# Moving the adds of the SwiGLU weight-block sums from VectorE to GpSimd in a hybrid conv/RWKV-7 trunk

## The chip, the cores and the metric

One core of a Trainium2 chip. The metric is the device time of one launch in microseconds, as the median of three runs. The kernel computes in 32-bit floats; large products run on TensorE as three passes over operands that are split in a high and a low part.

## The reference, cut to what matters

One layer (DEPTH = 1) over 2048 prompt tokens and 64 decode tokens. The part that the change touches belongs to the feed-forward network at the end:

```python
proj = jnp.einsum('btd,dc->btc', h, p["w_in"])            # input projection, 42 blocks of 128 columns
...
x = x + _rms_norm(m, p["norm_mix_post"])
h = _rms_norm(x, p["norm_ffn_pre"])
up = jnp.einsum('btd,df->btf', h, p["w_ffn_up"])
f = jnp.einsum('btf,fd->btd', jax.nn.silu(up[..., :D_FF]) * up[..., D_FF:], p["w_ffn_down"])
x = x + _rms_norm(f, p["norm_ffn_post"])
```

Between the projection and the feed-forward network stand a short gated convolution, an RWKV-7 recurrence over chunks of 64 tokens, and the merge of the two branches.

## The kernel before, in words

The kernel has two phases. Phase A (`phase_a`) makes the input projection and, woven into it, the RWKV-7 scan. The projection goes through the tokens in slices of 264 columns, two at a time; every weight block of `w_in` (128 x 1024 floats, 512 KB) is loaded by SP into `w_raw` (two buffers), cast by ACT into `w_hi` (L149) and reduced by DVE to `w_lo` (L150), and then used for 48 matrix products (8 row blocks, 3 passes, two token slices). What comes out of PSUM is worked on by ACT, DVE and POOL: in `rwkv_unit` POOL copies one column of history into the row tile `pr` (L303) and the last column back (L305), and DVE mixes each token with its predecessor (L307). The scan's three streams (`scan_prep`, `scan_solve`, `scan_chain`) use small DVE instructions (L759 and L761 solve triangular systems, L703, L704 and L715 make their inputs), 64-wide matrix products (`pu`, `pa`, `gy`, `tr`) and two POOL instructions for each group (L861, L862). Phase B merges the branches and runs the SwiGLU network.

The feed-forward products use a scheme with seven block products in the place of eight. Some of these need sums and differences of weight blocks. `weight_sums` makes them during phase A: for each of 34 jobs (22 of `w_up`, 12 of `w_down`) SP loads four blocks into the four buffers `sw` (L602), four adds in place make the four sums (L605), and SP stores them to the DRAM scratch `us_s` or `ds_s` (L609), from where phase B reads them. 88 of the 136 blocks belong to `w_up`; 120 adds have 512 columns, 16 have 384. The job's steps are called from `projections` through `sum_step`, from the 24th call on at every second call.

Nothing in the text fixes the final order: the framework's scheduler sets the rows of each engine from the written order, the buffers and its own estimates; on the chip each engine then works through its rows in that order, waiting on semaphores. SP's rows carry nearly all loads and stores of phase A, the weight blocks (L148), the loads and stores of the sums (L602, L609), the scratch stores (L380) and the scan's loads (L650) among them. A row that waits holds up all behind it on its engine.

Of the kernel before, what the change touches and what calls it, by code (L numbers as in the profile page):

```python
# [13 lines left out]
ALU = mybir.AluOpType  # L14
# [71 lines left out]
class Trunk:  # L86
# [500 lines left out]
    def weight_sums(self):  # L587

        nc = self.nc
        up, wd = self.i["w_up"], self.i["w_down"]  # L590
        jobs = [(lambda i, j, f=f: up[NF * i + f, :, HK * j:HK * j + HK, :], lambda s, f=f: self.us_s[s, f]) for f in range(NF)]
        for u in range(4):
            for k0, kn in KCHUNKS:
                jobs.append((lambda i, j, u=u, k0=k0, kn=kn: wd[2 * u + i, :, FH * j + k0:FH * j + k0 + kn, :],
                             lambda s, u=u, k0=k0, kn=kn: self.ds_s[s, u, :, k0 * P:(k0 + kn) * P]))
        for src, dst in jobs:
            w = {}
            for i in range(2):
                for j in range(2):
                    x = src(i, j)  # L600
                    w[i, j] = self.pa.tile([P, HK, P], F32, name="sw", bufs=4)[:, :x.shape[1]]
                    nc.sync.dma_start(out=w[i, j], in_=x)  # L602
            yield
            for n, (x, y) in enumerate((((1, 1), (1, 0)), ((1, 0), (0, 0)), ((0, 0), (1, 1)), ((0, 1), (0, 0)))):
                nc.vector.tensor_tensor(out=w[x], in0=w[x], in1=w[y], op=ALU.add)  # L605
                if n % 2:
                    yield
            for k, sm in (((1, 1), S_1), ((1, 0), S_3), ((0, 0), S_2), ((0, 1), S_4)):
                nc.sync.dma_start(out=dst(sm), in_=w[k].rearrange("p k c -> p (k c)"))  # L609
            yield  # L610
# [854 lines left out]
```

## Time and profile before

| | us |
|---|---|
| median of 3 runs (lowest to highest) | 3318.92 (3309.05 to 3333.54) |
| the profiled execution, its own time | 3331.18 |
| span of the profiled execution | 3329.4 |
| busy in the span: PE, DVE, ACT, POOL | 3145.9, 2497.7, 1663.1, 463.7 |
| mean granted TensorE clock | 0.974 of 2.4 GHz |

Times within the execution are microseconds from the start of the span. Phase A's projection and scan reach to about 1480 us; the sums lie between 26 and 1176 us. Busy times are unions; "idle before" and "waited for" name what ended a wait. The chain is the sequence of work and waits that ended last, followed back in time. The profiled execution lies 12 us above the median of the runs, so differences are worked out against 3331.18 and then put on 3318.92.

### The profile page before, as it was taken

How to read it: one execution, taken by the hardware profiler on the slowest of the kernel's cores; microseconds unless marked ns; L12 is line 12 of the kernel's file. 1: busy time of each engine (PE TensorE's matmuls, PEld its weight loads, DVE VectorE, ACT ScalarE, POOL GpSimd, SP SyncE). 2: the span in 40 equal slices, each digit the busy share in tenths (PEclk: the TensorE clock that was granted, in tenths of full speed). 3: DMA queues.
4: the chain of work that ended last, by engine and by line, in shares of the span. 5: the costliest groups of instructions: out<-in, count | busy, mean ns of one | idle time of the engine just before them, and what ended most of it. 6: DMA issues, size and time to landing. Idle time of an engine off the chain costs nothing.

```text
span 3329.4 us, 64336 instructions
## 1 busy us (share of the span) xinstructions
PE 3145.9 (94%) x23060; PEld 3061.0 (92%) x23060; DVE 2497.7 (75%) x5325; ACT 1663.1 (50%) x3246; POOL 463.7 (14%) x885
## 2 busy tenths in 40 slices
PE   5899998999989999998998999999999999999996
PEld 5889998988988899998998999999999999999996
DVE  6776887888778876745486788886878887877766
ACT  6534664565476445443434355346544456444453
POOL 2310022032013100000010011210012200111100
PEclk9999999999999999999999999999999999999998
DMA  7787677766675655547475467778767777766674
GB/s 259 239 247 228 203 245 235 246 195 210 175 237 164 205 147 172 157 141 228 126 229 162 137 218 235 259 224 269 231 220 239 248 246 240 234 191 192 194 233 147
DMA packets 534833, 699.52 MB, mean 210 GB/s; under 512 B 112672, under 2 KB 368224, under 8 KB 534512
## 3 DMA queue, kind: packets, MB, share of 16 engines
q1 hardware_dynamic: 478880, 597.27, 59.1%
q0 software_dynamic: 24000, 67.61, 5.4%
q10 hardware_dynamic: 31632, 30.53, 2.7%
q8 instruction: 181, 2.97, 0.4%
q14 instruction: 140, 1.15, 0.1%
HBM read 522.10 MB, written 173.12 MB: 209 GB/s over the span
## 4 chain that ended last, share of the span: by engine, by line
issue 42%; PE 35%; DMA 8%; DVE 7%; POOL 5%; ACT 2%; SPq 0%; POOLq 0%; ACTq 0%; DVEq 0%
PE mm L136 28%; PE pu L136 4%; POOL tp_s L1214 3%; PE gy L136 2%; DMA w_raw<-in_w_in 1%; DVE w_lo L150 1%; PE tr L140 1%; DMA x<-in_x 1%; POOL x_s L1085 1%; DMA lo_s<-ks 1%; POOL out_y L1085 1%; DVE sw L605 1%; PE pa L136 1%; DVE ti L761 1%; DMA ka<-lo_s 1%
## 5 line engine op out<-in xcount | busy, mean ns | idle before, releaser
L136 PE MATMUL mm<-h_hi,w_hi 128*128 128x264 f32 (+1 forms) x5112 | 1594.9, 312 | 53.5 <-DVE f L1233 22.7
L136 PE MATMUL mm<-h_lo,w_hi 128*128 128x264 f32 (+1 forms) x5112 | 1567.2, 307 | 4.3 <-DVE h_lo L217 3.6
L136 PE MATMUL mm<-h_hi,w_lo 128*128 128x264 f32 (+1 forms) x5112 | 1563.5, 306 | 7.0 <-DVE w_lo L150 7.0
L136 PEld LDWEIGHTS mm<-h_hi,w_hi 128*128 128x128 f32 x5112 | 978.9, 192 | 80.9 <-DVE f L1233 26.8
L136 PEld LDWEIGHTS mm<-h_lo,w_hi 128*128 128x128 f32 x5112 | 981.3, 192 | 9.4 <-DVE h_lo L217 4.7
L136 PEld LDWEIGHTS mm<-h_hi,w_lo 128*128 128x128 f32 x5112 | 980.7, 192 | 8.8 <-DVE w_lo L150 7.8
L188 ACT CAST w_hi<-w_raw 128x512 fp32r<-128x512 f32 (+1 forms) x810 | 485.7, 608 | 587.9 <-PE mm L136 435.1
L189 DVE TENSOR_TENSOR w_lo<-w_raw,w_hi 128x512 fp32r<-128x512 f32 (+1 forms) x810 | 540.6, 674 | 145.8 <-ACT w_hi L188 140.4
L136 PE MATMUL mm<-t_hi,w_hi 128*128 128x352 f32 x1116 | 361.1, 324 | 0.6 <-ACT o L1058 0.6
L136 PE MATMUL mm<-t_hi,w_lo 128*128 128x352 f32 x1116 | 358.3, 321 | 0.0
L136 PE MATMUL mm<-t_lo,w_hi 128*128 128x352 f32 x1116 | 358.2, 321 | 0.0
L150 DVE TENSOR_TENSOR w_lo<-w_raw,w_hi 128x1024 fp32r<-128x1024 f32 x168 | 208.3, 1240 | 96.6 <-ACT w_hi L149 94.6
L149 ACT CAST w_hi<-w_raw 128x1024 fp32r<-128x1024 f32 x168 | 175.8, 1047 | 157.5 <-PE mm L136 126.5
L136 PEld LDWEIGHTS mm<-t_hi,w_hi 128*128 128x128 f32 x1116 | 209.4, 188 | 1.3 <-ACT o L1058 0.8
L136 PEld LDWEIGHTS mm<-t_lo,w_hi 128*128 128x128 f32 x1116 | 209.9, 188 | 0.3
L136 PEld LDWEIGHTS mm<-t_hi,w_lo 128*128 128x128 f32 x1116 | 209.4, 188 | 0.0
L1214 POOL DMA_DIRECT2D tp_s<-f x231 | 124.9, 541 | 574.4 <-DVE f L1233 327.9
L189 DVE TENSOR_TENSOR t_lo<-d,t_hi 128x352 fp32r<-128x352 f32 x198 | 97.6, 521 | 85.7 <-ACT t_hi L188 85.1
L188 ACT CAST t_hi<-d 128x352 fp32r<-128x352 f32 x198 | 90.9, 485 | 110.5 <-DMA d<-tp_s 103.8
L1233 DVE TENSOR_TENSOR f<-mm,f 128x352 f32<-128x352 f32 x198 | 103.1, 521 | 47.7 <-PE mm L136 47.4
L759 DVE TENSOR_TENSOR tm<-al,ti 128x60 f32<-128x60 f32 (+27 forms) x527 | 118.7, 225 | 17.1 <-DMA ti<-in_eye 5.1
L761 DVE TENSOR_TENSOR ti<-ti,tm 128x60 f32<-128x60 f32 (+27 forms) x527 | 123.7, 235 | 9.8
(198 smaller groups left out, 3747.3 us busy)
## 6 DMA issues: line engine op xcount, KB each, us to landing
w_raw<-in_w_in SPq DMA_DIRECT2D x168, 512.0 KB, 4.3
w_raw<-us_s SPq DMA_DIRECT2D x264, 256.0 KB, 3.1
w_raw<-in_w_up SPq DMA_DIRECT2D x198, 256.0 KB, 3.4
tp_s<-f POOLq DMA_DIRECT2D x231, 176.0 KB, 3.6
d<-tp_s SPq DMA_DIRECT2D x105, 352.0 KB, 4.0
w_raw<-ds_s SPq DMA_DIRECT2D x96, 256.0 KB, 3.7
sw<-in_w_up SPq DMA_DIRECT2D x88, 256.0 KB, 4.4
us_s<-sw SPq DMA_DIRECT2D x88, 256.0 KB, 3.7
```

The source lines that it names most:

```text
L136: self.nc.tensor.matmul(out, lhsT, rhs, **kw)
L140: self.nc.tensor.transpose(out, in_, ident)
L149: nc.scalar.copy(out=hi[:, :kt], in_=raw[:, :kt])
L150: nc.vector.tensor_tensor(out=lo[:, :kt], in0=raw[:, :kt], in1=hi[:, :kt].bitcast(F32), op=ALU.subtract)
L188: nc.scalar.copy(out=hi, in_=x)
L189: (eng or nc.vector).tensor_tensor(out=lo, in0=x, in1=hi.bitcast(F32), op=ALU.subtract)
L605: nc.vector.tensor_tensor(out=w[x], in0=w[x], in1=w[y], op=ALU.add)
L759: nc.vector.tensor_tensor(out=tv, in0=al[0:np_, u, u + 1:32].unsqueeze(1).broadcast_to([np_, k, m]), in1=ti[0:np_, 0:k, u:u + 1].broadcast ...
L761: nc.vector.tensor_tensor(out=tu, in0=tu, in1=tv, op=ALU.add)
L1085: (nc.sync if tail else nc.gpsimd).dma_start(out=dst[d, :, t0:t0 + n], in_=x)
L1214: nc.gpsimd.dma_start(out=self.tp_s[TP[op], i], in_=x)
L1233: nc.vector.tensor_tensor(out=out, in0=x, in1=y, op=op)
```

## The change

The adds of L605 are issued on POOL (GpSimd) and no longer on DVE (VectorE):

```diff
             for n, (x, y) in enumerate((((1, 1), (1, 0)), ((1, 0), (0, 0)), ((0, 0), (1, 1)), ((0, 1), (0, 0)))):
-                nc.vector.tensor_tensor(out=w[x], in0=w[x], in1=w[y], op=ALU.add)
+                nc.gpsimd.tensor_tensor(out=w[x], in0=w[x], in1=w[y], op=ALU.add)
                 if n % 2:
                     yield
```

The scheduler answers with another order on every engine. On POOL, at the start of phase A (`acc` and `hf` belong to the norm of the second token slice, `pr` is the row tile, `sw` the sums):

```order
 L184 TENSOR_TENSOR acc<-acc,psv 128x264 x7
+L605 TENSOR_TENSOR sw<-sw 128x512 x4
 L215 TENSOR_TENSOR hf<-kbk,rs 128x264 x2
...
-L215 TENSOR_TENSOR hf<-al,rs 128x264 x3
...
+L215 TENSOR_TENSOR hf<-al,rs 128x264 x2
+L605 TENSOR_TENSOR sw<-sw 128x512
+L215 TENSOR_TENSOR hf<-al,rs 128x264
+L605 TENSOR_TENSOR sw<-sw 128x512 x3
+L305 COPY pr_hist<-pr 128x1
```

The first four adds now stand between the sums of squares and the scaling of the second slice, and the next four ahead of the first copies of history.

On SP, at the same place, before:

```order
L194 DMA x<-in_x 128x2x264 x3
L609 DMA us_s<-sw 128x512
L148 DMA w_raw<-in_w_in 128x1024 x2
L609 DMA us_s<-sw 128x512 x3
L602 DMA sw<-in_w_up 128x512 x4
L296 DMA ka<-lo_s 128x264
```

and on SP after the change:

```order
L194 DMA x<-in_x 128x2x264 x3
L609 DMA us_s<-sw 128x512 x4
L602 DMA sw<-in_w_up 128x512 x2
L148 DMA w_raw<-in_w_in 128x1024 x2
L602 DMA sw<-in_w_up 128x512 x2
L609 DMA us_s<-sw 128x512 x4
```

The pair of weight loads that stood behind one store of a sum stands behind four stores and two of the next loads.

On POOL in the later part of the first passes (`cc` is the decay that the state update reads, `tinv` the inverse of the solve), before:

```order
L772 MEMSET tinv 32x16x32
L724 COPY cc<-ep 128x4 x2
L665 MEMSET ep 128x8
L861 TENSOR_TENSOR ysq<-ysq,bv 128x512
L862 TENSOR_TENSOR ysq<-ysq,g 128x512
```

and after the change:

```order
L772 MEMSET tinv 32x16x32
L861 TENSOR_TENSOR ysq<-ysq,bv 128x512
L862 TENSOR_TENSOR ysq<-ysq,g 128x512
L605 TENSOR_TENSOR sw<-sw 128x512 x12
L724 COPY cc<-ep 128x4
L605 TENSOR_TENSOR sw<-sw 128x512 x2
L724 COPY cc<-ep 128x4
```

Here the adds of three jobs stand in one run ahead of a copy that the state update waits for. Over the whole program all 136 adds stand on POOL, in 49 rows, 15 of them runs of four; of the 168 loads of `w_in` blocks, 101 stand ahead of the last store of a sum on SP, where 132 did.

## Rows read from the trace of the kernel before

**Rows 1.** Busy time by stretch: us, PE, PEld, DVE, ACT, POOL (instructions), clock, DMA, GB/s.
```profile
0.00:166.00 166.00, 123.80 (x877) 117.15 (x878) 117.41 (x193) 101.31 (x209) 51.31 (x95) 0.95 0.77 249
166.00:500.00 334.00, 317.53 (x2840) 304.01 (x2839) 249.66 (x607) 173.87 (x320) 44.05 (x89) 0.97 0.75 231
500.00:832.00 332.00, 309.79 (x2701) 295.12 (x2699) 281.94 (x688) 188.05 (x375) 79.20 (x146) 0.95 0.73 221
832.00:1210.00 378.00, 356.11 (x3222) 337.20 (x3221) 292.85 (x783) 204.36 (x409) 71.09 (x161) 0.95 0.64 192
1210.00:1480.00 270.00, 268.82 (x2473) 257.12 (x2472) 182.42 (x470) 141.12 (x247) 15.01 (x20) 1.00 0.52 154
```

**Rows 2.** What PE waited for from 45 to 1210 us: total, times, longest.
```profile
PE tr L140 <- DMA v<-v_s: 14.5, 3, 8.1
PE pu L136 <- DVE aa L715: 13.1, 16, 2.3
PE pa L136 <- DVE v L704: 11.0, 7, 2.4
PE mm L136 <- DVE w_lo L150: 7.0, 4, 3.8
```

**Rows 3.** Line 605: durations in ns (min/median/max), and DVE's idle time ahead of it.
```profile
L605 DVE TENSOR_TENSOR sw<-sw x136: 543/684/1791, 25.9 to 1175.7; 128x512 f32<-128x512 f32 x120, 128x384 f32<-128x384 f32 x16
...
  DMA sw<-in_w_up: 11.0, 5
...
  DMA sw<-in_w_down: 2.5, 1
```

**Rows 4.** The chain that ended last, from 0 to 1210 us, shares by line.
```profile
by line: PE mm L136 41.1%; PE pu L136 8.4%; issue 5.8%; PE gy L136 3.1%; DMA w_raw<-in_w_in 2.4%; DVE w_lo L150 2.2%; PE tr L140 1.9%; DMA lo_s<-ks 1.8%; DMA x<-in_x 1.8%; DVE sw L605 1.7%; DVE ti L761 1.6%; DMA ka<-lo_s 1.6%; DMA us_s<-sw 
```

**Rows 5.** POOL's instruction groups over the span: busy us, mean ns, idle before.
```profile
L861 POOL TENSOR_TENSOR ysq<-ysq,bv 128x512 f32<-128x512 f32 (+1 forms) x17 | 24.1, 1415 | 189.7 <-ACT ysq L860 115.9 <-PE mm L136 62.3 <-DVE sw L605 11.4
L862 POOL TENSOR_TENSOR ysq<-ysq,g 128x512 f32<-128x512 f32 (+1 forms) x17 | 23.8, 1402 | 1.3
```

**Rows 6.** Timeline from 363.5 us: start, us, engine, line, operation.
```profile
363.76 0.19 DVE L761 TENSOR_TENSOR ti<-ti,tm 128x28 f32<-128x28 f32 x1
...
364.06 1.29 POOL L861 TENSOR_TENSOR ysq<-ysq,bv 128x512 f32<-128x512 f32 x1 [14.09 <-ACT ysq L860]
...
364.20 1.19 DVE L761 TENSOR_TENSOR ti<-ti,tm 128x24 f32<-128x24 f32 x1
...
365.43 1.31 POOL L862 TENSOR_TENSOR ysq<-ysq,g 128x512 f32<-128x512 f32 x1
...
365.64 1.13 DVE L761 TENSOR_TENSOR ti<-ti,tm 128x16 f32<-128x16 f32 x1
```

**Rows 7.** What SP's queue waited for from 0 to 1210 us: total, times, longest.
```profile
SPq L609 <- DVE sw L605: 42.8, 34, 8.7
SPq L602 <- DMA us_s<-sw: 26.3, 29, 5.4
SPq L609 <- DVE tm L759: 22.4, 19, 3.8
```

**Rows 8.** Timeline of SP's issues from 24 us.
```profile
26.58 0.34 SPq L609 DMA_DIRECT2D us_s<-sw  x1
29.12 1.47 SPq L148 DMA_DIRECT2D w_raw<-in_w_in  x2
33.78 0.33 SPq L609 DMA_DIRECT2D us_s<-sw  x1
```

**Rows 9.** Timeline of POOL from 12 us.
```profile
14.56 6.22 POOL L184 TENSOR_TENSOR acc<-acc,psv 128x264 f32<-128x264 f32 x7 [11.96 <-ACT psv L183]
27.04 2.62 POOL L215 TENSOR_TENSOR hf<-kbk,rs 128x264 f32<-128x264 f32 x2 [6.26 <-DVE h_lo L217]
```

**Rows 10.** What DVE waited for from 0 to 1210 us, the two largest that name POOL.
```profile
DVE psv L307 <- POOL pr_hist L305: 6.3, 4, 2.2
...
DVE psv L307 <- POOL pr L303: 1.5, 2, 1.2
```

**Rows 11.** DMA issues: KB each, median us from issue to landing.
```profile
us_s<-sw SPq DMA_DIRECT2D x88, 256.0 KB, 3.7
```

## The prediction, made before the changed kernel ran

> **What bounds the kernel now.** I read the busy times by stretch first, because the adds that move lie between 26 and 1176 us [rows 3] and only that part can change at once. In each of the four stretches up to 1210 us PE is the busiest engine, and DVE comes second; POOL works a third of the time at most [rows 1]. PE's idle time there is 42.2 + 16.5 + 22.2 + 21.9 = 103 us (length less busy time, [rows 1]), of which 42 us belong to the start-up. In the next stretch, without sums, PE waits 1.2 us of 270. The clock column says that idle time has a second price: 1.00 where PE does not wait, 0.95 to 0.97 where it does [rows 1], that is, some slices run at 1.2 GHz in the place of 2.4. Weighted over 1210 us the mean is 0.955, so some 54 us of full-speed time are not granted beside 103 us idle. I therefore count every us by which PE's waits grow or shrink as 1.5 us.
>
> Second, what PE waits for: after the start-up the largest entries that DVE ends are 13.1, 11.0 and 7.0 us, the masks of the scan, its scaled keys and the low parts of the weights [rows 2]. DVE is thus what stands behind much of PE's waiting, but it ends a few waits of 2 us each; it does not feed PE all the time. Third, how much of this is the sums: on the chain that ended last up to 1210 us, line 605 has 1.7% [rows 4], 20.6 us, of the 136 x 0.684 = 93 us that the adds take [rows 3]. So 22% of the adds' time lay where it counted; with this share I turn DVE time into time at PE.
>
> **What is removed.** 136 adds leave DVE, 93 us. With them goes the idle time in which DVE stood at an add whose load had not landed, 11.0 + 2.5 = 13.5 us [rows 3]. DVE's load up to 1210 us is 942 us (the sum of four stretches, [rows 1]), so this is a ninth of it.
>
> **What is added on POOL.** The nearest rows are POOL's two operations of the same shape, 1415 and 1402 ns in the mean [rows 5] (one of the 17 is half as wide, so these are a little low). 120 x 1.41 + 16 x 1.06 (three quarters as wide) = 186 us. POOL's 246 us in this part become 432 us of 1210, 36%: room enough for the work, and the question is only who waits for it.
>
> **What the two engines do to each other.** The trace of before shows the case in small. A solver instruction of 0.19 us, begun while POOL ran an operation of 1.29 us, took 1.19 us and ended with it, at 365.39 against 365.35; the same happened beside the next operation, 1.13 us [rows 6]. The add itself has a median of 684 ns and a maximum of 1791 ns [rows 3]. So one POOL operation can cost DVE up to 1791 - 684 = 1.1 us, and it costs nothing where DVE reads PSUM or waits anyway. The ends are 0 and 136 x 1.1 = 150 us. I take the half, 75 us, since the rows show both: the adds' median is far nearer to their minimum than to their maximum, and the solver's short instructions are caught whole.
>
> The Trainium skill, SBUF — State Buffer, section "Who interferes with whom", speaks against this change: a VectorE instruction with two inputs in SBUF and a GpSimd instruction that reads SBUF exclude each other for a whole instruction. These rows agree, 1.19 us beside 0.19. By that rule the upper end would hold wherever DVE's next instruction has two inputs in SBUF; what it would make of the sum is the second rival below.
>
> DVE's balance is then -93 - 13.5 + 75 = -31 us, and at PE 22% of it, -7 us.
>
> **What waits for POOL instead.** The stores of the sums, on SP. SP waited 42.8 us for an add itself and 22.4 us for a solver instruction that stood ahead of one on DVE [rows 7]. Each add is 1.41 - 0.69 = 0.72 us longer, 98 us in all; what stands behind the stores on SP are the loads of `w_in` blocks. Bounds: if the weights are ahead as far as now, nothing; if PE's waits for weights (7.0 us, [rows 2]) grow in proportion to the two waits on SP (65 us), 7.0 / 65 x 98 = 10.5 us. I take 4 us, nearer to nothing, since PE waited only four times for weights although SP waited 34 and 19 times. The buffers' turn-round (store, landing of 3.7 us [rows 11], load) stays as it is and is waited for on SP now too, 26.3 us [rows 7].
>
> At the start the place is certain. Two weight loads went out at 29.12 behind one store [rows 8]. Now four stores and two loads stand ahead: POOL is done with the sums of squares at 20.8 [rows 9], the four adds end at 20.8 + 5.6 = 26.4, a store lands 3.7 later, at 30.1, the two loads take 1.5 to issue as the two at 29.12 did: 31.6, so 2.5 us late. The scaling that now stands behind these adds began at 27.04 [rows 9], after 26.4, and loses nothing.
>
> Last, the copies of history: DVE waited 6.3 + 1.5 us for them [rows 10]. POOL's load grows by 1.76, so about 6 us more, if the copies only suffer from more load; bounds are 0 and, with half a run of four adds (2.8 us) at each of 34 jobs, 95 us. I take 9 us of DVE's time, near the proportional figure, and 22% of it, 2 us.
>
> **The sum.** -7 + 4 + 2.5 + 2 = +1.5 us at PE, times 1.5 = +2 us. Against the profiled execution that is 3331.2 + 2 = 3333; on the median of the runs, 3318.9 + 2 = 3321 us. The two halves cancel, so the sign is open; between the ends of the terms (DVE's balance from -106 to +44, the stores from 0 to 10.5, the copies from 0 to 21 at PE) the likeliest case has a range of its own of 3295 to 3350. One per cent, 33 us, is about what a measurement of this kernel can tell from no change.
>
> **Rivals.**
> First, faster: the engines rarely meet. For it speaks that the adds' median is 684 ns and that their work can slide into POOL's idle time; the whole 20.6 us of the chain and half of the 13.5 us then go, 27.4 us, less the late weights at the start, 2.5: 25 x 1.5 = 37 us, 3282 us. Against it: both POOL operations of [rows 6] caught a DVE instruction.
>
> Second, the exclusion in full (the upper end): DVE loses 150 us and gains 106, +44 us, 22% of which is +10 at PE in the place of -7. With the other terms 10 + 8.5 = 18.5, x 1.5 = 28 us: 3347 us. For it speak the solver's 31 steps of two such instructions in each of 17 groups, all of two inputs; against it that DVE is idle a fifth of the time.
>
> Third, slower, and by the queue on SP alone: the stores of each job wait 4 x 0.72 = 2.9 us longer, and weight loads stand right behind. If half of that reaches PE in each of 34 jobs, 1.45 x 34 = 49 us, x 1.5 = 74, less 10 for DVE's relief: 3383 us. It decides from 0.2 us a job on (0.2 x 34 x 1.5 = 10, the relief). For it speaks the order at the start, where weights have moved behind four stores; against it that PE waited for weights 7.0 us in all.
>
> That the change does not do what it says can be left aside: all adds stand on POOL in the new order.
>
> **Chances.** Forecast 0.48, first rival 0.15, second 0.18, third 0.19. Faster by over 1% (below 3286) is over half of the first rival and a little of the forecast: 0.11. Slower by over 1% (above 3352) is most of the third, 0.16, two fifths of the second, 0.07, and 0.02 of the forecast: 0.25. Within 1% remains 0.64. The range, 3283 to 3378 us, leaves out about half of the first rival and half of the third, 0.17.
>
> **What would show it.** Right: line 605 on POOL at 1.4 us and more; solver and mixing instructions on DVE longer in the mean; DVE's busy time up to 1210 us down by 93 - 75, about 20 us, and not by 93; SP's waits for the adds about doubled; PE's idle time up to 1210 us within 10 us of 103. The first rival would show DVE's busy time down by 80 or more and PE's waits for masks and keys halved; the second DVE's busy time up; the third long waits of SP's stores for POOL and of PE for `w_lo` or of ACT for `w_raw`. The forecast is wrong if PE's idle time up to 1210 us moves by over 20 us either way, or if phase B, which the change does not touch, moves the end.

## The result and the profile after

The changed kernel takes 3366.76 us, median of 4 runs (3365.31 to 3378.46), against 3318.91 us of the kernel before on the same chip: ratio 1.0162, 95% interval 1.0137 to 1.0186. The medians are 48 us apart, and the ratio of the runs puts the step at 54 us: slower by over 1%. The profiled execution took 3378.46 us (span 3376.7, clock 0.969), 47 us more than that of before, so the two traces show the difference.

The busy times by stretch (columns as in [rows 1]) of the changed kernel:

```profile
0.00:166.00 166.00, 119.35 (x805) 112.65 (x806) 109.96 (x154) 98.35 (x200) 89.80 (x119) 0.92 0.76 248
166.00:500.00 334.00, 305.24 (x2617) 292.28 (x2617) 250.48 (x536) 159.85 (x294) 108.41 (x127) 0.93 0.72 223
500.00:832.00 332.00, 294.35 (x2506) 279.67 (x2504) 269.87 (x559) 176.01 (x353) 120.24 (x180) 0.94 0.70 217
832.00:1210.00 378.00, 353.04 (x3263) 334.43 (x3263) 307.14 (x790) 208.14 (x427) 97.30 (x186) 0.97 0.62 185
1210.00:1480.00 270.00, 267.05 (x2459) 254.34 (x2458) 187.58 (x520) 133.17 (x227) 15.88 (x30) 0.98 0.52 149
```

PE's idle time up to 1210 us is 46.7 + 28.8 + 37.7 + 25.0 = 138 us, where it was 103. The clock column falls with it; weighted by length, 1210 us now lose 68 us to the lower clock level where they lost 54. So 35 us of waiting and, as an estimate from a column of two decimals, 14 us of clock make 49 us: the whole loss lies here. Phase A agrees: its last weight block is reduced (L150) by 1555.3 us where it was 1501.3, and what follows takes 7 us less than before. Counted in matrix products, the changed kernel is 72 behind at 166 us, 72 + 223 = 295 at 500, 490 at 832 and 449 at 1210. The lag is built while the sums run densely and is not caught up.

The sums themselves, by line (durations min/median/max, first and last start), and then the page's groups (busy us, mean ns of one, idle time before and what ended it) for the sums and for the three DVE lines named below, of the changed kernel and then of the kernel before:

```profile
L605 POOL TENSOR_TENSOR sw<-sw x136: 991/1292/2304, 22.0 to 949.7; 128x512 f32<-128x512 f32 x120, 128x384 f32<-128x384 f32 x16
```

```profile
L150 DVE TENSOR_TENSOR w_lo<-w_raw,w_hi 128x1024 fp32r<-128x1024 f32 x168 | 217.8, 1297 | 113.2 <-ACT w_hi L149 109.1
...
L605 POOL TENSOR_TENSOR sw<-sw 128x512 f32<-128x512 f32 (+1 forms) x136 | 190.6, 1401 | 170.3 <-DMA sw<-in_w_up 94.6
...
L761 DVE TENSOR_TENSOR ti<-ti,tm 128x60 f32<-128x60 f32 (+27 forms) x527 | 141.2, 268 | 12.4
L759 DVE TENSOR_TENSOR tm<-al,ti 128x60 f32<-128x60 f32 (+27 forms) x527 | 140.9, 267 | 21.7 <-DMA ti<-in_eye 6.7
```

```profile
L150 DVE TENSOR_TENSOR w_lo<-w_raw,w_hi 128x1024 fp32r<-128x1024 f32 x168 | 208.3, 1240 | 96.6 <-ACT w_hi L149 94.6
...
L759 DVE TENSOR_TENSOR tm<-al,ti 128x60 f32<-128x60 f32 (+27 forms) x527 | 118.7, 225 | 17.1 <-DMA ti<-in_eye 5.1
L761 DVE TENSOR_TENSOR ti<-ti,tm 128x60 f32<-128x60 f32 (+27 forms) x527 | 123.7, 235 | 9.8
```

An add takes 1401 ns in the mean on POOL, 190.6 us in all. On DVE the solver's instructions went from 225 and 235 ns to 267 and 268, the low parts of the weights from 1240 to 1297. Over all DVE groups that both kernels share (the lines up to 1090 without the sums and without phase B's L189; 2998 instructions in either kernel) the busy time rose from 1406.7 to 1501.1 us, by 94.4 us. The adds that left DVE had taken 94.0 us. DVE was relieved of nothing: what it gave to POOL it got back as longer instructions. That the two figures meet is chance; with 48 adds moved (below), 32 us went and 35 came back. The lengthening stands beside the adds: the 188 DVE instructions of phase A that overlap one in time are 102 us longer in all than the short ones of the same form, the tenth percentile over all the traces, while those that meet no POOL work but its small copies and memsets are 25 us longer, with 26 in the kernel before.

The timeline of DVE and POOL at one job shows how (start, us, engine, line, operation, rows that repeat joined):

```profile
271.42 0.20 DVE L759 TENSOR_TENSOR tm<-al,ti 128x48 f32<-128x48 f32 x1
...
271.54 5.35 POOL L605 TENSOR_TENSOR sw<-sw 128x512 f32<-128x512 f32 x4 [14.67 <-DMA sw<-in_w_up]
...
271.65 1.21 DVE L761 TENSOR_TENSOR ti<-ti,tm 128x48 f32<-128x48 f32 x1
...
272.90 1.35 DVE L759 TENSOR_TENSOR tm<-al,ti 128x69 f32<-128x69 f32 x1
...
274.29 1.32 DVE L761 TENSOR_TENSOR ti<-ti,tm 128x69 f32<-128x69 f32 x1
...
275.64 1.33 DVE L759 TENSOR_TENSOR tm<-al,ti 128x66 f32<-128x66 f32 x1
...
277.00 0.23 DVE L761 TENSOR_TENSOR ti<-ti,tm 128x66 f32<-128x66 f32 x1
```

POOL's four adds end at 276.89. In these 5.35 us DVE gets four solver instructions through, one for each add, each about as long as the add beside it; ahead of the run and behind it one takes 0.20 and 0.23 us. This is what [rows 6] had shown twice in small.

Such stalls stand in chains that others wait for. The chain that ended last, up to 1210 us, answers to [rows 4]:

```profile
by line: PE mm L136 28.6%; issue 6.2%; PE pu L136 6.0%; DVE ti L761 4.7%; DVE tm L759 4.4%; DVE w_lo L150 3.6%; POOL sw L605 2.3%; DMA lo_s<-ks 2.1%; PE tr L140 2.0%; DVE psv L307 2.0%; PE gy L136 2.0%; ACT w_hi L149 1.8%; DMA w_raw<-in_w_i
```

L761 went from 1.6% to 4.7%; L759 (behind the end of the row of before, where it had 1.4%) to 4.4%; `w_lo` from 2.2% to 3.6%. Line 605 itself kept its place on the chain, 2.3% where it had 1.7%, now as POOL's. What PE waited for from 45 to 1210 us answers to [rows 2] (total, times, longest):

```profile
PE pa L136 <- DVE v L704: 15.0, 6, 5.3
...
PE mm L136 <- ACT ks L434: 10.8, 4, 5.8
PE mm L136 <- ACT psv L306: 9.3, 7, 2.5
...
PE pu L136 <- DVE aa L715: 5.9, 11, 1.3
...
PE mm L136 <- DVE w_lo L150: 1.9, 2, 1.1
```

No single entry holds the 35 us. The wait for the masks (`aa`) fell; that for the scaled keys (`v`) rose from 11.0 to 15.0, its longest from 2.4 to 5.3 us; `ks` and `psv`, which come out of the mixing, stand at 10.8 and 9.3. The wait for weights, in which a delay by SP's queue would show, fell from 7.0 to 1.9 us.

SP and DVE as waiters, answering to [rows 7] and [rows 10], and the start, answering to [rows 8] and [rows 9]:

```profile
SPq L609 <- POOL sw L605: 133.2, 69, 10.5
...
SPq L609 <- POOL pr_hist L305: 16.3, 10, 6.0
...
SPq L602 <- DMA us_s<-sw: 12.3, 12, 3.1
```

```profile
DVE psv L307 <- POOL pr_hist L305: 4.2, 2, 2.7
...
DVE psv L307 <- POOL pr L303: 1.3, 2, 1.0
```

```profile
32.45 1.48 SPq L148 DMA_DIRECT2D w_raw<-in_w_in  x2
```

```profile
22.03 5.55 POOL L605 TENSOR_TENSOR sw<-sw 128x512 f32<-128x512 f32 x4 [0.82 <-DMA x<-in_x]
...
30.37 2.62 POOL L215 TENSOR_TENSOR hf<-kbk,rs 128x264 f32<-128x264 f32 x2 [2.79 <-DVE h_lo L217]
```

SP's stores wait 133.2 us for POOL's adds, twice the 42.8 + 22.4 us of before and a little more; ten other waits (16.3 us) name a copy of history that stands ahead of an add on POOL. Counted whole, up to 1210 us, the stores of the sums wait 164 us where they waited 100, but the loads of the next blocks 14 where they waited 54, and all waits of SP together come to 773 us where they were 760. Much of the waiting changed its place on SP. DVE waits less for POOL's copies, not more. The first two weight loads go out at 32.45, 3.3 us late, and the scaling of the second slice starts 3.3 us late as well, released by DVE.

### The profile page after: what moved, and what is told of

It reads as the page before. It is cut to its first block, busy times and chain, and to the rows that moved or that the text cites. A ratio compares the mean times of both kernels' runs of the same rounds, so it can differ in the third digit from the quotient of the medians.

```text
span 3376.7 us, 64369 instructions
## 1 busy us (share of the span) xinstructions
PE 3160.5 (94%) x23060; PEld 3072.7 (91%) x23060; DVE 2528.2 (75%) x5189; ACT 1661.4 (49%) x3242; POOL 639.1 (19%) x1021
## 4 chain that ended last, share of the span: by engine, by line
issue 41%; PE 31%; DVE 12%; DMA 7%; POOL 7%; ACT 3%; SPq 0%; POOLq 0%; DVEq 0%; ACTq 0%
PE mm L136 25%; PE pu L136 3%; POOL tp_s L1214 3%; DVE ti L761 2%; DVE tm L759 2%; DVE w_lo L150 1%; PE gy L136 1%; PE tr L140 1%; POOL sw L605 1%; DMA lo_s<-ks 1%; DVE psv L307 1%; ACT w_hi L149 1%; POOL out_y L1085 1%; DMA w_raw<-in_w_in 1%; POOL x_s L1085 1%
## 5 line engine op out<-in xcount | busy, mean ns | idle before, releaser
L189 DVE TENSOR_TENSOR w_lo<-w_raw,w_hi 128x512 fp32r<-128x512 f32 (+1 forms) x810 | 541.6, 675 | 152.5 <-ACT w_hi L188 145.4
L150 DVE TENSOR_TENSOR w_lo<-w_raw,w_hi 128x1024 fp32r<-128x1024 f32 x168 | 217.8, 1297 | 113.2 <-ACT w_hi L149 109.1
L605 POOL TENSOR_TENSOR sw<-sw 128x512 f32<-128x512 f32 (+1 forms) x136 | 190.6, 1401 | 170.3 <-DMA sw<-in_w_up 94.6
L759 DVE TENSOR_TENSOR tm<-al,ti 128x60 f32<-128x60 f32 (+27 forms) x527 | 140.9, 267 | 21.7 <-DMA ti<-in_eye 6.7
L189 DVE TENSOR_TENSOR t_lo<-d,t_hi 128x352 fp32r<-128x352 f32 x198 | 97.9, 522 | 73.8 <-ACT t_hi L188 73.5
L761 DVE TENSOR_TENSOR ti<-ti,tm 128x60 f32<-128x60 f32 (+27 forms) x527 | 141.2, 268 | 12.4
```

The source lines that it names most:

```text
L150: nc.vector.tensor_tensor(out=lo[:, :kt], in0=raw[:, :kt], in1=hi[:, :kt].bitcast(F32), op=ALU.subtract)
L189: (eng or nc.vector).tensor_tensor(out=lo, in0=x, in1=hi.bitcast(F32), op=ALU.subtract)
L605: nc.gpsimd.tensor_tensor(out=w[x], in0=w[x], in1=w[y], op=ALU.add)
L759: nc.vector.tensor_tensor(out=tv, in0=al[0:np_, u, u + 1:32].unsqueeze(1).broadcast_to([np_, k, m]), in1=ti[0:np_, 0:k, u:u + 1].broadcast ...
L761: nc.vector.tensor_tensor(out=tu, in0=tu, in1=tv, op=ALU.add)
```

## The experiments

Two theories were set against each other. **Exclusion:** a POOL instruction that reads SBUF stops DVE instructions with two inputs in SBUF, and these stalls are the loss. **Queue:** POOL's adds are twice as long, so the stores on SP wait, and what stands behind them comes late. Ratios are against the kernel before on the same chip, with 95% intervals; medians of before were 3306.24 us for the first four kernels, 3303.27 for the next four and 3309.98 for the last four. Expectations were worked out against 3319, so a measured ratio is the fairer comparison. Edits are shown against the kernel before.

**No adds at all**, as the base for both sides.

```diff
-                nc.vector.tensor_tensor(out=w[x], in0=w[x], in1=w[y], op=ALU.add)
+                pass
```

> The adds of line 605 are left out on every engine; loads and stores of the blocks stay, so the sums that phase B reads are plain blocks. It measures what the adds cost at all, whichever engine makes them. Both theories, the exclusion (a POOL add holds up every DVE instruction that reads two tiles in SBUF) and the queue (longer adds hold up SP's stores and what stands behind them), expect less than the kernel before: by the chain's 20.6 us and its share of clock at most 31 us, so 3288 to 3318 us. DVE's busy time up to 1210 us about 93 us below before. If it is not faster than before, DVE's relief was worth nothing at PE even without any price.

Measured: 3289.65 us, ratio 0.9947 (0.9932 to 0.9962). Freeing DVE of 94 us of adds and of the waits at their head is worth 17 us of the end, 0.19 us for each us of adds. A change of engine could hardly have gained more than that.

**POOL busy, but only writing.** Three memsets in the place of each add.

```diff
-                nc.vector.tensor_tensor(out=w[x], in0=w[x], in1=w[y], op=ALU.add)
+                for part in (w[x], w[x], w[x][:, :2]):
+                    nc.gpsimd.memset(part, 0.0)
```

> In the place of each add POOL writes zeros into the block, in three memsets (two and a half widths, about 1.3 us by the 524 ns of a 128x512 memset), so POOL is occupied for as long as by the adds and the stores wait as long, but POOL reads nothing; the sums are left out. Exclusion: as without adds, within 10 us of that run, 3285 to 3325 us, and the solver's instructions on DVE at their length of before (225 and 235 ns in the mean, against 267 and 268 with POOL's adds). Queue: as slow as with the adds on POOL, 3350 to 3375 us.

Measured: 3305.75 us, ratio 0.9993 (0.9982 to 1.0003), 172 us of memsets on POOL, and SP's stores waiting 82.8 us for them (133.2 for the adds of the change). The queue theory fails as the main cause: most of POOL's time is there and more than half of SP's waits, the loss is not. Against the kernel without adds there remain 15 us that occupation and waits may cost, more than the 10 that were expected. The timeline of this kernel beside four memsets:

```profile
235.49 1.83 POOL L606 MEMSET sw<- 128x512 f32 x4 [0.74 <-DMA sw<-in_w_up]
...
235.53 0.19 DVE L760 TENSOR_TENSOR tm<-al,ti 128x28 f32<-128x28 f32 x1
...
235.98 0.18 DVE L760 TENSOR_TENSOR tm<-al,ti 128x24 f32<-128x24 f32 x1
```

The same instructions that take 1.21 to 1.35 us beside adds take 0.18 and 0.19 us here. The 2998 shared DVE instructions take 1402.8 us, no more than before. The Trainium skill, SBUF — State Buffer, section "Who interferes with whom", makes this very distinction: a VectorE instruction with two SBUF inputs contends with a GpSimd instruction that reads SBUF, and not with one that only writes it. Both rows agree with it.

One kind of instruction is held by memsets, too, and it has a single tile as input: L368, a `tensor_scalar` on `hf`, with a median of 298 ns in this kernel. Here one stands beside a run of memsets, and no other POOL work, from 105.97 to 109.38 us:

```profile
106.81 1.74 DVE L368 TENSOR_SCALAR hf<-hf 128x264 f32<-128x264 f32 x1
```

There are only 32 of these, and beside memsets they lose 2.4 us in all; in the change one took 1.39 us beside adds, at 528.52.

**Both: the sums stay on DVE, POOL adds beside them** into a tile of its own that nobody waits for.

```diff
                 nc.vector.tensor_tensor(out=w[x], in0=w[x], in1=w[y], op=ALU.add)
+                nc.gpsimd.tensor_tensor(out=self.dm[:, :w[x].shape[1]], in0=self.dm[:, :w[x].shape[1]], in1=w[x], op=ALU.add)
```

> DVE makes the adds as before, and POOL adds each sum once more into a private tile that nothing reads: the exclusion alone, with the stores waiting for DVE as before. Exclusion: DVE's instructions lose about as much as with the adds on POOL (their busy time up to 1210 us fell by 4 us where 93 left, so about 89 us), with no relief: slower than the changed kernel, 3375 to 3420 us. Queue: as before, within 10 us of 3319 us.

Measured: 3403.43 us, ratio 1.0293 (1.0275 to 1.0311). Its groups of the solver:

```profile
L762 DVE TENSOR_TENSOR tm<-al,ti 128x60 f32<-128x60 f32 (+27 forms) x527 | 148.7, 282 | 16.6 <-DMA ti<-in_eye 4.8 <-DMA al<-asc 2.3
L764 DVE TENSOR_TENSOR ti<-ti,tm 128x60 f32<-128x60 f32 (+27 forms) x527 | 148.7, 282 | 9.8
```

The sums are made where they were and no engine gives up work, yet 136 adds on POOL (213.7 us) that serve nothing cost 97 us. The shared DVE instructions take 104 us more and the adds 12 us more. The rows of DVE, ACT and PE stand in the same order as in the kernel before, instruction for instruction, so no new order has a part in this. It is the exclusion's price with nothing to set against it, except that SP's stores wait longer for the lengthened DVE (133 us in all, where it was 100). The private tile could keep the four `sw` buffers busy longer, but SP's waits at the loads into them fell from 54 to 39 us.

**Adds on POOL, and the stores issued from POOL too**, so that SP waits for no add.

```diff
-                nc.vector.tensor_tensor(out=w[x], in0=w[x], in1=w[y], op=ALU.add)
+                nc.gpsimd.tensor_tensor(out=w[x], in0=w[x], in1=w[y], op=ALU.add)
...
-                nc.sync.dma_start(out=dst(sm), in_=w[k].rearrange("p k c -> p (k c)"))
+                nc.gpsimd.dma_start(out=dst(sm), in_=w[k].rearrange("p k c -> p (k c)"))
```

> Adds on POOL as in the changed kernel, but their stores are issued by POOL too, behind the adds, so that SP never waits for an add. Exclusion: still slow, 3350 to 3385 us. Queue: back near 3319 us, 3305 to 3335, with SP free of the 133 us of waits for line 605.

Measured: 3419.52 us, ratio 1.0344 (1.0329 to 1.036): slower than the change, outside what either theory expected. What SP waits for in this kernel:

```profile
SPq L602 <- DMA us_s<-sw: 119.8, 40, 12.2
```

The waits did not leave SP; its next loads of sum blocks now wait for the stores, 119.8 us where it was 12.3. The sums also end at 763 us in the place of 950, so the stalls come closer together, and POOL spends 76 us on issuing the 136 stores, 0.56 us each. The run does not tell the theories apart; it only shows that taking the stores off SP is no remedy.

**Copies in the place of adds**: POOL reads one tile, not two.

```diff
-                nc.vector.tensor_tensor(out=w[x], in0=w[x], in1=w[y], op=ALU.add)
+                nc.gpsimd.tensor_copy(out=w[x], in_=w[y])
```

> In the place of each add POOL copies the block w[y] into w[x]: one tile read, not two; the sums are left out. It asks whether it is POOL's reading that costs, or its reading of two tiles. If any reading shuts DVE's two-input instructions out, the run is slower than the one with memsets by the share that the copy's length has of the add's: with a copy at 0.7 of the add's 1.40 us about 38 us above the memsets' ratio of 0.999, so 3330 to 3360 us where the kernel before has 3319, and solver instructions again of over 1 us beside POOL's. If only two-tile reading costs, it is like the memsets, 3300 to 3325.

Measured: 3303.13 us, ratio 0.999 (0.9975 to 1.0005): no loss, a miss for the exclusion as I had put it. The timeline shows that copies do stop the solver:

```profile
221.78 2.97 POOL L605 COPY sw<-sw 128x512 f32<-128x512 f32 x3
221.83 0.63 DVE L761 TENSOR_TENSOR ti<-ti,tm 128x64 f32<-128x64 f32 x1
...
222.50 0.65 DVE L759 TENSOR_TENSOR tm<-al,ti 128x75 f32<-128x75 f32 x1
```

Each stalled instruction lasts as long as one copy (614 ns in the median). In all the shared DVE instructions take 1437.6 us, 31 more than before, 0.23 us for each copy where it is 94.4 / 136 = 0.69 for each add. A third of the lengthening, in stalls half as long, leaves the kernel level with the memsets, where the shared instructions are no longer than before. Why it costs so little is not settled (below).

This kernel is also the closest match of the change. On DVE, ACT, POOL, PE and SP its rows stand in the same order, instruction for instruction (buffer numbers aside); only the 136 rows of L605 differ. So the scheduler's new order alone is not the loss: with copies it runs level with the kernel before. From copies to adds, in one order, the kernel loses 1.7%, some 57 us, with 63.5 us more of stalls. POOL's time (191 us for 98) and the waits of SP's stores (164 us for 113) grow along with them, so this pair alone does not part the two theories.

**Only the 48 sums of `w_down` on POOL.** They run from 602 us on, so the start-up stays as it was.

```diff
-                nc.vector.tensor_tensor(out=w[x], in0=w[x], in1=w[y], op=ALU.add)
+                eng = nc.gpsimd if (src, dst) in jobs[NF:] else nc.vector
+                eng.tensor_tensor(out=w[x], in0=w[x], in1=w[y], op=ALU.add)
```

> Only the adds of the 12 jobs of w_down (48 of 136) are made by POOL, those of w_up by DVE. If the price is per add, wherever it stands, 48 / 136 of the changed kernel's 1.62% remain: 0.57%, 3319 x 1.0057 = 3338 us. If it hangs on the start-up and the dense first part (the changed kernel's lag in matrix products is built up before 832 us), where w_up's jobs lie, it is within 0.2% of before, 3312 to 3326 us.

Measured: 3341.45 us, ratio 1.0098 (1.007 to 1.0125). Its adds by line:

```profile
L606 POOL TENSOR_TENSOR sw<-sw x48: 984/1290/2267, 601.9 to 984.2; 128x512 f32<-128x512 f32 x32, 128x384 f32<-128x384 f32 x16
```

Both expectations were missed. With 35% of the adds comes 60% of the loss (43 to 77% by the interval), so the loss is not one of the start alone, and it does not go by the count of adds either. Up to 1210 us PE is idle for 120.5 us, 18 us more than before.

**The reverse: POOL's own two-tile operations to DVE**, the adds staying on DVE as before.

```diff
-            nc.gpsimd.tensor_tensor(out=bv, in0=bv, in1=x, op=ALU.mult)
+            nc.vector.tensor_tensor(out=bv, in0=bv, in1=x, op=ALU.mult)
...
-        nc.gpsimd.tensor_tensor(out=ks[:, 1], in0=ks[:, 0], in1=a, op=ALU.mult)
+        nc.vector.tensor_tensor(out=ks[:, 1], in0=ks[:, 0], in1=a, op=ALU.mult)
...
-        nc.gpsimd.tensor_tensor(out=yr, in0=yr, in1=bv, op=ALU.add)
-        nc.gpsimd.tensor_tensor(out=yr, in0=yr, in1=g, op=ALU.mult)
+        nc.vector.tensor_tensor(out=yr, in0=yr, in1=bv, op=ALU.add)
+        nc.vector.tensor_tensor(out=yr, in0=yr, in1=g, op=ALU.mult)
```

> The other way round: the adds stay on DVE, and POOL's own two-input operations of phase A (lines 332, 371, 861 and 862, 32 + 32 + 17 + 17 instructions, about 113 us on POOL) are made by DVE, about 50 us there (64 x 0.43 + 34 x 0.69). Exclusion: DVE is rid of what these cost it beside its own work; by the run with POOL's extra adds (97 us for 214 us of POOL, 0.45 us per us) that is some 50 us of the whole, and DVE's 50 us more cost about 50 x 17.5 / 94 = 9 us: faster than before by 15 to 45 us, 3275 to 3305. If exclusion costs only where POOL's adds stand in rows of four, DVE's load decides: 3320 to 3340 us.

Measured: 3258.33 us, ratio 0.9849 (0.9823 to 0.9875), the fastest of all: 1.5% faster than the kernel before, 3% faster than the changed one, and a little better than either expectation. Its busy times by stretch and its solver groups:

```profile
0.00:166.00 166.00, 131.18 (x956) 125.72 (x956) 128.80 (x229) 109.04 (x225) 49.96 (x89) 0.95 0.82 271
166.00:500.00 334.00, 323.09 (x2936) 309.76 (x2937) 259.28 (x642) 177.97 (x339) 29.38 (x78) 0.99 0.74 234
500.00:832.00 332.00, 318.98 (x2911) 304.04 (x2911) 277.71 (x738) 185.18 (x358) 46.16 (x109) 0.98 0.72 221
832.00:1210.00 378.00, 365.50 (x3332) 345.90 (x3332) 297.55 (x844) 218.78 (x433) 46.88 (x130) 0.98 0.68 203
```

```profile
L759 DVE TENSOR_TENSOR tm<-al,ti 128x60 f32<-128x60 f32 (+27 forms) x527 | 109.2, 207 | 10.7 <-DMA ti<-in_eye 2.0
L761 DVE TENSOR_TENSOR ti<-ti,tm 128x60 f32<-128x60 f32 (+27 forms) x527 | 109.2, 207 | 9.0
```

DVE is busier up to 1210 us than in the kernel before (963 us against 942, [rows 1]), and still PE is idle for 71 us in the place of 103. POOL's load there falls from 246 to 172 us, the solver's mean from 225 and 235 ns to 207. DVE, the second busiest engine, got 50 us of work that had taken 113 us on POOL, and the 2998 shared instructions became 43 us shorter. How much of the gain is due to these shorter stalls and how much to the moved operations ending sooner was not separated.

**Only the tail of each scan group to DVE** (L861 and L862, 48 us of POOL, [rows 5]).

```diff
-        nc.gpsimd.tensor_tensor(out=yr, in0=yr, in1=bv, op=ALU.add)
-        nc.gpsimd.tensor_tensor(out=yr, in0=yr, in1=g, op=ALU.mult)
+        nc.vector.tensor_tensor(out=yr, in0=yr, in1=bv, op=ALU.add)
+        nc.vector.tensor_tensor(out=yr, in0=yr, in1=g, op=ALU.mult)
```

> Only lines 861 and 862 (34 instructions, 48 us on POOL, about 23 us on DVE) go to DVE; 332 and 371 stay on POOL. Exclusion: 48 x 0.45 = 22 us less, 23 x 0.19 = 4 us more: 3295 to 3312 us. Otherwise 3315 to 3330.

Measured: 3285.98 us, ratio 0.9931 (0.9908 to 0.9955), solver 210 and 216 ns. A little under half of the gain with 34 instructions, within what was expected.

**Adds on POOL in pieces of 128 columns**, so that a stall ends sooner.

```diff
-                nc.vector.tensor_tensor(out=w[x], in0=w[x], in1=w[y], op=ALU.add)
+                for k in range(w[x].shape[1]):
+                    nc.gpsimd.tensor_tensor(out=w[x][:, k], in0=w[x][:, k], in1=w[y][:, k], op=ALU.add)
```

> Adds on POOL, but each in four instructions of 128 columns (three for the narrow ones). By POOL's instructions of 264 and 512 columns (0.745 and 1.28 us undisturbed) a piece takes about 0.45 us, a sum of four pieces 1.8 us. The runs with copies (0.61 us each, no loss against memsets) and with whole adds (1.29 us, 54 us of loss) suggest that a stall is what is left of POOL's instruction when DVE arrives, so that short ones cost little: 3310 to 3340 us. If the price goes by POOL's reading time in all, it grows with it, 3370 to 3400 us.

Measured: 3377.01 us, ratio 1.0199 (1.0181 to 1.0218). Its group of adds, and SP's two largest waits at the stores:

```profile
L606 POOL TENSOR_TENSOR sw<-sw 128x128 f32<-128x128 f32 x528 | 275.8, 557 | 192.2 <-DMA sw<-in_w_up 112.6 <-DMA sw<-in_w_down 33.6 <-DMA ttsc<-ti 19.0
```

```profile
SPq L610 <- POOL sw L606: 149.6, 92, 4.5
SPq L610 <- DMA sw<-in_w_up: 53.5, 15, 8.0
```

The stalls halve (shared DVE instructions 1451.8 us, 45 more than before in the place of 94), but the kernel is no faster than the change: it came out where the second expectation, a price by POOL's reading time, had put it. The adds now take 275.8 us, a sum 2.2 us, and SP waits 203 us at the stores. So short pieces are no remedy; that SP's waits took back what the shorter stalls gave is argued from these rows, not shown.

**Solver out of the way.** A base kernel in which the solver's state `ti` stands in PSUM, so that L759 and L761 have one input in SBUF only, and its match with the adds on POOL.

```diff
-        ti = pool.tile([P, 8, 32], F32, name="ti", bufs=1)
-        nc.sync.dma_start(out=ti[0:np_], in_=self.i["eye" if nch == 2 else "eye1"])
+        te = pool.tile([P, 8, 32], F32, name="te", bufs=1)
+        nc.sync.dma_start(out=te[0:np_], in_=self.i["eye" if nch == 2 else "eye1"])
         yield 6
+        ti = self.psum.tile([P, 8, 32], F32, name="ti", bufs=1)
+        nc.scalar.copy(out=ti[0:np_], in_=te[0:np_])
...
+        nc.scalar.copy(out=te[0:np_], in_=ti[0:np_])
...
-            k.mmbufs = 4
+            k.mmbufs = 3
```

> A base for the next run: adds on DVE as before, but the solver's tile ti (lines 759 and 761) lies in PSUM, so each of its 1054 instructions has one input in SBUF and one in PSUM; PSUM has three banks for the projection in the place of four. If the solver's stalls beside POOL's own operations cost time, the solver's instructions are never over 1 us and the run gains up to some 20 us; one bank less may cost as much: 3290 to 3345 us.

> The same with the adds on POOL. If the price is paid in the solver's serial chain (it carries 9.1% of the chain up to 1210 us in the changed kernel where it had 3.0%), POOL's adds cost at most 0.5% against the base with ti in PSUM: within 17 us of it. If it is paid by all two-input instructions alike (the solver's share of DVE's lengthening is some four tenths), 0.9% to 1.2% remain: 30 to 40 us above it.

Measured: the base 3315.49 us, ratio 1.0009 (0.9991 to 1.0028); with the adds on POOL 3378.21 us, ratio 1.0208 (1.019 to 1.0226). The step between them is 1.0208 / 1.0009 = 1.020, no less than the change itself. The groups of the second kernel:

```profile
L150 DVE TENSOR_TENSOR w_lo<-w_raw,w_hi 128x1024 fp32r<-128x1024 f32 x168 | 223.4, 1331 | 109.6 <-ACT w_hi L149 106.1 <-DMA ttsc<-te 2.2 <-PE mm L136 0.5
...
L763 DVE TENSOR_TENSOR ti<-ti,tm 128x60 f32<-128x60 f32 (+27 forms) x527 | 111.8, 212 | 9.4
L761 DVE TENSOR_TENSOR tm<-al,ti 128x60 f32<-128x60 f32 (+27 forms) x527 | 106.1, 201 | 39.8 <-ACT ti L756 30.4
L307 DVE SCALAR_TENSOR_TENSOR psv<-pr,cpack,psv 128x264 f32<-128x264 f32 (+2 forms) x126 | 70.7, 564 | 26.5 <-ACT psv L306 13.3 <-POOL pr_hist L305 6.5 <-POOL pr L303 4.0
```

and the solver's in the base:

```profile
L763 DVE TENSOR_TENSOR ti<-ti,tm 128x60 f32<-128x60 f32 (+27 forms) x527 | 111.2, 211 | 7.3
L761 DVE TENSOR_TENSOR tm<-al,ti 128x60 f32<-128x60 f32 (+27 forms) x527 | 105.4, 200 | 36.3 <-ACT ti L756 29.4 <-DMA al<-asc 0.3
```

The solver is untouched by POOL: with one input in PSUM its instructions are not held. The stalls are in others: `w_lo` 1331 ns where it was 1248 in the base, mixing 564 where it was 479. The shared DVE instructions took 75.7 us more than in the base. A theory that the price is paid in the solver's chain alone is refuted. The other expectation, 0.9 to 1.2%, was missed as well: with less lengthening than in the change the loss is larger. The mixing and the weights, too, have PE behind them; PE's wait for L306, ACT's step ahead of the mixing, is 28.8 us where it was 10.0 in the base.

**The change on top of the reverse**: POOL's other two-tile work on DVE, the adds on POOL, so that no add stands in a queue with it.

```diff
-                nc.vector.tensor_tensor(out=w[x], in0=w[x], in1=w[y], op=ALU.add)
+                nc.gpsimd.tensor_tensor(out=w[x], in0=w[x], in1=w[y], op=ALU.add)
```

(beside the four lines of the reverse, above)

> The best kernel so far (lines 332, 371, 861 and 862 on DVE, 0.985 of before) with the adds on POOL: POOL then reads two tiles for the sums alone. If the price is per add, 0.985 x 1.016 = 1.001 of before, 3322 us; if it comes from POOL's queue, where adds and the other operations hold each other up, nearly nothing is added: 0.985 to 0.992, 3269 to 3292 us. If DVE's load were what counts, it gains once more: below 0.98.

Measured: 3345.25 us, ratio 1.0104 (1.0088 to 1.0119). Against the reverse alone that is 1.0104 / 0.9849 = 1.026: the adds cost more here than in the change, not less, and more than either expectation. The shared DVE instructions and the moved ones (3096) went from 1413.6 to 1508.5 us, by 94.9, the same 0.70 us for each add as in the change. So the price of the adds does not come from the other two-tile work in POOL's queue.

The runs together (PE idle up to 1210 us, worked out from the busy times as above; "shared DVE" is the busy time of the 2998 instructions):

| kernel | ratio | PE idle | shared DVE, us over before |
|---|---|---|---|
| POOL's two-tile work on DVE | 0.9849 | 71 | -43 |
| its tail alone on DVE | 0.9931 | 85 | -26 |
| no adds | 0.9947 | 90 | -1 |
| copies on POOL | 0.999 | 101 | +31 |
| memsets on POOL | 0.9993 | 98 | -4 |
| before | 1 | 103 | 0 |
| solver's state in PSUM | 1.0009 | 89 | -17 |
| 48 adds on POOL | 1.0098 | 121 | +35 |
| adds on POOL, its other two-tile work on DVE | 1.0104 | 116 | +45 |
| **the change** | 1.0162 | 138 | +94 |
| adds on POOL in pieces | 1.0199 | 145 | +45 |
| adds on POOL, solver's state in PSUM | 1.0208 | 133 | +59 |
| adds on both | 1.0293 | 152 | +104 |
| adds and stores on POOL | 1.0344 | 166 | +117 |

The idle times are of the one execution that was profiled; that of before lies 12 us above its median, so its 103 is rather high beside the others. PE's idle time goes with the ratios in the main; out of line are chiefly the two kernels with the solver's state in PSUM. DVE's lengthening alone does not order them: the pieces cost more than their 45 us would say, and the copies less than their 31.

## Why the prediction was right or wrong, point by point

**Where the time is lost** came out as said: PE's idle time and clock up to 1210 us hold it, phase B nothing. The factor of 1.5 was a little high; 48 us of the end for 35 us of idle time make 1.4.

**The size.** +2 us was forecast, +48 came: inside the range, on the side that had a chance of 0.25. By the text's own sign of failure, PE's idle time moving by over 20 us (it moved by 35), the likeliest case was wrong; its own range ended at 3350 (the ends of its terms, added up, reach 3384). That 3366.76 lies inside the stated range is in part luck: the upper end stood as high as 3378 for the third rival's sake, a wait by SP's queue, and that is not what happened. The second rival, the exclusion in full (3347), named the direction and the mechanism but not what came: its sign was DVE's busy time going up, and up to 1210 us that went from 942 to 937 us. It put the stalls at 150 us where 94 were measured, nearer to the forecast's 75. What was too low in both is the price of a us of stall at PE.

**The step that failed** is "DVE's balance is then -93 - 13.5 + 75 = -31 us, and at PE 22% of it, -7 us". It failed twice. First, 75 us was too little: 94 us was measured, 0.69 us for each add in the place of 0.55, inside the bounds of 0 and 1.1. Alone this would have made the balance -12 us and the sum some 6 us more. Second, and this is most of it, one share was used for two different things. The 22% came from the adds as fillers; the kernel without adds confirms it in kind (17 us of the end for 94 us, 0.19, where 22% times 1.5 had made 0.33). But a stall does not strike fillers. It strikes whatever two-input instruction DVE has next, in the solver's steps, the mixing and the low parts of weights, which others wait for. Against the kernel without adds the change adds some 94 us to the shared instructions and 48 + 17 = 65 us to the end, 0.69 us for each; if the 15 us that the memsets cost are taken off as occupation and waits, 0.53. A us of stall cost about three times what a us of removed work gave. The kernel with adds on both engines, where nothing is relieved, makes it 97 us for 116. The price is no constant: by the ratios, with the same relief of 17 us (for 48 adds, their share of it), it is 1.1 us in each of the kernels with 48 adds, with the solver's state in PSUM and on top of the reverse, 0.9 from copies to adds, and 0.4 from no adds to copies.

**The stores on SP.** That SP's waits for adds would about double was right (65 to 133 us). The price of 4 us was too much rather than too little: PE's waits for `w_lo` fell. The third rival, by the queue alone, fell with the memsets, which make SP wait 82.8 us at no loss, and with the adds on both engines, where POOL holds up no store and 97 us are lost. In the kernel with pieces the queue may have a part.

**The start.** The weight loads were put at 31.6 and went out at 32.45. That the scaling "loses nothing" was wrong: it began 3.3 us late, behind DVE and not behind the adds. The lag of 72 products at 166 us is more than these 2.5 us account for, but the kernel with 48 adds from 602 us on shows that much of the loss needs no start.

**The copies of history.** 2 us were put in; DVE's waits for them fell from 7.8 to 5.5 us [rows 10]. Nothing here.

**POOL's add** was taken at 1.41 us from [rows 5] and 186 us in all; 1.40 and 190.6 were measured.

**The first rival**, that the engines rarely meet, is refuted by the shared instructions. Its price for the relief (37 us) was twice what the kernel without adds gives.

**What stays open.** Copies stop DVE as well, 31 us in all, and the kernel with them stands level with the memsets, while the pieces lengthen DVE by 45 us and lose 2%. The number of tiles that POOL reads, the length of a stall, the total POOL time (98 us against 191 and 276) and the waits of SP are not separated, nor is it shown why a us of stall costs from 0.4 to 1.1 us of the end. Two copies for each add, the same POOL time with one input, were not tried.

## What to carry to other kernels

An idle POOL is no free room for work that reads two tiles (copies cost nothing that could be measured here): before work goes there, look which two-input DVE instructions will run beside it and who waits for them. Where the rows show a short DVE instruction that ends with a POOL one, the reverse is the change to try, even onto a DVE that is busy 78% of the time: here it was worth 1.5%. Price removed work by its own share of the chain, but price a stall by what stands behind the instruction that it holds.

## What the runs showed of the hardware that was not expected

- In a run of POOL adds DVE gets one two-input instruction through for each add: 1.21, 1.35, 1.32 and 1.33 us beside four adds of 5.35 us.
- Memsets on POOL do not hold the solver's two-input instructions (0.18 and 0.19 us beside them), but did hold a `tensor_scalar` with one tile as input (1.74 us where the median is 0.30); copies hold a two-input instruction for one copy's length (0.63 and 0.65 us); a DVE instruction with one of its inputs in PSUM is not held beside adds (solver 201 and 212 ns, 200 and 211 without them).
- 94.0 us of adds moved off DVE came back as 94.4 us of longer instructions; on top of the reverse, with another order of the rows, 91.6 us as 94.9.
- POOL's add in pieces of 128 columns takes 557 ns in the mean, 275.8 us for what 136 whole adds do in 190.6.
